# A hybrid SSD and attention layer: other places for the first conv's taps and softplus, the scan's tokens loaded ahead, the pre-norm's gains ahead of the first weights

## The chip, the cores and the metric

The kernel runs on one core of a Trainium2 chip. The core has a matrix engine (TensorE, PE), a vector engine (VectorE, DVE), a scalar engine (ScalarE, ACT), a general engine (GpSimd, POOL) and a queue engine (SyncE, SP) that here issues the transfers (DMAs). PEld is PE's loading of weights, which overlaps its matmuls. The metric is the device time of one execution in microseconds (us), as the median of several runs; lower is better. The clock in the profile is the one granted to TensorE, as a share of full speed.

## The reference

One layer on 16 learned meta tokens and 1024 tokens, width 1024, float32 throughout:

```python
h = concat([meta, x])
xn = rms_norm(h, mix_pre_g)
proj = xn @ w_in                      # z, xbc, dt_raw, q, k, v
y_ssd = ssd_mixer(z, xbc, dt_raw, ...)
y_sb = rms_norm(stick_breaking_attention(q, k, v), sb_norm_g)
h = h + rms_norm(concat([y_ssd, y_sb]) @ w_out, mix_post_g)
gu = rms_norm(h, ffn_pre_g) @ w_up
f = (gelu(causal_dwconv(gu[:DFF])) * gu[DFF:]) @ w_down
out = (h + rms_norm(f, ffn_post_g))[16:]
```

and in the mixer, which the change touches:

```python
xbc = silu(causal_dwconv(xbc, conv_w, conv_b))    # 4 taps; x (1024), B and C (2 groups of 128)
dt = softplus(dt_raw + dt_bias)
# over chunks of 128 tokens: y = (C.B^T * decay) @ (x dt) + C @ state,
# state = state * decay + B^T @ (x dt * decay), then y = (y + x*D) * silu(z)
```

## The kernel before

**Number format and products.** Every float32 operand is split into a high part (`h`, by a copy on ACT into the rounded matmul type) and a low part (`l`, the remainder, by a subtraction on POOL or DVE). Each product of two operands is then three matmuls, high by high, high by low, low by high.

**Stages.** The program runs through a head (normalise the tokens, turn them so that width lies on the partitions, and project B and C of group 0 and dt), a stage of projections in blocks, the scan over chunks, the attention, the output projection and the feed-forward part. PE's order, and with it that of DVE, ACT and POOL, is the order in which the code is written; SP is scheduled automatically in the stage of projections, and in written order in the head and the scan.

**The head** (L330 to L470). SP loads in order: the meta tokens `xt0`, `xt1`, the weights of B (`wr_B`, 512 KB), the pre-norm's gains spread over the partitions (`gpre`), `xt2`, `xt3`, and so on. For each tile of tokens `square` (ACT, L359) gives the sum of squares, `root` (POOL, L169 and L170) the factor `rs_pre`, `norm` (DVE, L369) the tile `xn`, and `turn_x` (PE, L383) its eight transposes `xtp`, which ACT copies (high part) and DVE subtracts (low part). `split_hi` (ACT, L415) and `split_lo` (DVE, L419) split B's weights between `norm(1)` and `square(2)`.

**The projections** (class `Duo`, L258 to L321). A duo is two blocks of 128 columns of the weights, for 1040 tokens, in Strassen's manner: seven products numbered 1, 6, 5, 7, 2, 3, 4 instead of eight, each of 24 matmuls (L308), in three banks of accumulators `dA`, `dX`, `dY`. Product 7 adds into the bank of product 6, product 3 into that of 5, product 2 into that of 1. After each product its bank is added or copied out to the raw tiles `craw`, by ACT for products 1 and 2 (L317), by DVE for the others (L320, "evacuation" below). The first duo is of x columns (`x`), then comes one of z, then x, z, then B and C of group 1, and so on. The first duo takes its products in the order 1, 5, 2, 6, 7, 3, 4. While a duo runs, the weights of the next one are made ready, each step behind a certain product: `split_1` (`whi1`, `wlo1`) behind 2, `split_22` (`ah`, `al`) behind 1, `sums` (four operations on POOL, L285 to L288) behind 6, `split_3` behind 7, `split_4` (`whi4`, `wlo4`) behind 3. In `split_w` (L178) the high part is on ACT, L181, and the low part on POOL, L182.

**Slots.** `slots` is a list of lists: what is in `slots[j]` is issued behind the j-th product of the running duo. In it go the work on B and C of group 0 and on dt: the four taps of the conv on DVE (tap 0 is the TENSOR_SCALAR of L505, taps 1 to 3 the SCALAR_TENSOR_TENSOR of L508) with a silu on ACT (L512) as fifth entry (`b0_taps`, `c0_taps`; tiles `cdB`, `cdC`), the turning of B into tokens by PE and ACT (`b0_turns`, L491 and L496), and the seven actions `dts`: loads of dt's parameters, `turn_dt` (PE, `tpd`), `soft_a` (softplus: e = exp on ACT, then s and s2 on DVE, L659 to L664), `soft_b` (its series on DVE), three decays and their stores. The last x operands `t2l`, `t3l` and `t4l` are split on DVE (L255) in the same time.

**The scan** (L1192 to L1230). There are 18 units, 9 chunks by 2 groups. Unit n computes the weights of unit n+1 and the outputs of unit n: `sg` (segment sums, PE L1070, from the loads `sl` and `sg`), `em` (ACT and later DVE and POOL L1100), `xdt` and `xw` (POOL, L1075 and L1080, from the token tile `xk`), `cb` (PE), `yf`, `st` (PE L1120, from `xw`), `yt` (PE L1136), and on DVE `xd` and `zk` (L1145, L1146), the outputs, which SP stores as `yd` (L1149). Projections of q and k (`pj_q`, `pj_k`, L218) fill PE between. At the head of each unit SP is given: stores of the q and k projections (`put_stores`, n < 2), the group's B and C (`load_state`, n = 0, 2, 6, 10), `zk` and `xd` of unit n+1 (L1056 and its like; a buffer of `zk` is free when its store as `yd` is done), `sl` and `sg` of unit n+3 (`load_bc`), and `xk` of unit n+2 (L1048).

Of the kernel before, what the change touches and what calls it, by code (L numbers as in the profile page):

```python
# [9 lines left out]
F32 = mybir.dt.float32  # L10
# [3 lines left out]
ALU = mybir.AluOpType  # L14
# [52 lines left out]
def tile_layer(ctx: ExitStack, tc: tile.TileContext, x, meta, rows, parts,  # L67
# [190 lines left out]
    class Duo:  # L258
# [13 lines left out]

        def split_22(self):
            h, l = (weight_rows(sa.tile([P, 5 * P], F32R, tag=f"a22{e}", name=f"a{e}{self.nm}", bufs=2), 4, OFF22)
                    for e in "hl")
            raw = self.r[1][:, HI4]
            nc.scalar.activation(h, raw, AF.Copy)
            nc.gpsimd.tensor_tensor(l, raw, h.bitcast(F32), op=ALU.subtract)
            self.w["a22"] = h, l
# [44 lines left out]
    with tc.tile_pool(name="pre", bufs=3, side="right") as pre:  # L324
# [13 lines left out]
        load_x(1)  # L338
        raws = {"B0": raw_of("B0", w_xbc[8])}
        gpre = row_bcast(pre, 0, D, "gpre")  # L340
        load_x(2)
        load_x(3)
        raw_dt = pre.tile([P, KB, 16], F32, tag="wdt", name="wr_dt", bufs=1)
# [81 lines left out]
        norm(1)  # L425
        split_hi("B0")
        split_lo("B0")
        square(2)
        root(2)
        norm(2)  # L430
        turn_x(0)
        square(3)
        root(3)
# [191 lines left out]
    def dt_acts():  # L625
# [30 lines left out]
        def soft_a():  # L656
            dtx = box["dtx"]
            e, s, s2 = box["e"], box["s"], box["s2"] = [t3(n) for n in ("e1", "s1", "s2")]
            nc.vector.scalar_tensor_tensor(e, dtx, -1.0, dtx, op0=ALU.mult, op1=ALU.min)  # L659
            nc.scalar.activation(e, e, AF.Exp)  # L660
            nc.vector.tensor_scalar(s, e, 2.0, None, op0=ALU.add)
            nc.vector.reciprocal(s, s)
            nc.vector.tensor_tensor(s, s, e, op=ALU.mult)
            nc.vector.tensor_tensor(s2, s, s, op=ALU.mult)  # L664
# [39 lines left out]
        def store():  # L704
            nc.sync.dma_start(out=dtkd, in_=dtk)

        return [[loads], [turn_dt], [soft_a], [soft_b], [lambda: decay(0)], [lambda: decay(1)],
                [lambda: decay(2), store, turn_acs]]
# [31 lines left out]
    def merged(*lists):  # L740
# [3 lines left out]
    dts = dt_acts()  # L744
    slots = [b0_taps[:2] + dts[0], b0_taps[2:4], b0_taps[4:], [], c0_taps[:2] + b0_turns[:1],
             c0_taps[2:4] + b0_turns[1:2], c0_taps[4:] + b0_turns[2:], dts[1]]
    for i, q in enumerate(duos):
# [3 lines left out]
        for j, m in enumerate((1, 5, 2, 6, 7, 3, 4) if i == 0 else (1, 6, 5, 7, 2, 3, 4)):  # L751
# [6 lines left out]
            if n is not None:  # L758
                if m == 1:
                    n.split_22()  # L760
                elif m == 6:
                    n.sums()
                elif m == 7:
                    n.split_3()
                elif m == 2:
                    n.split_1()
                elif m == 3:
                    n.split_4()
            elif m in (7, 2):
                v_split(1, int(m == 2))  # L770
# [6 lines left out]
        if i == 1:  # L777
            slots = merged(slots, [[], dts[2], [], dts[3], [], [], []]) + [dts[4], dts[5], dts[6]]
        if i == n_early:
# [220 lines left out]
    with tc.tile_pool(name="ssd", bufs=1, side="right") as sp:  # L1000
# [191 lines left out]
        for n, (g, c) in enumerate(units):  # L1192
            if n == 12:
                for d, u in zip(vcd, (vd, vdp)):
                    nc.sync.dma_start(out=d.rearrange("(t r) c -> t r c", r=NM),
                                      in_=u[P:].rearrange("(t r) c -> t r c", r=P)[:, :NM])
            if n < 2:
                put_stores()
            if n in (0, 2, 6, 10):
                load_state(n // 2 + 2, n // 2 + (4 if n else 3))  # L1200
            if n + 1 < len(units):
                load_zx(*units[n + 1])
            if n + 3 < len(units):
                load_bc(*units[n + 3])
            if n + 2 < len(units):
                load_x(*units[n + 2])
            nxt = chunk_weights(*units[n + 1]) if n + 1 < len(units) else None
# [1288 lines left out]
```

## Time and profile before

| what | us |
|---|---|
| median of three runs | 1659.45 |
| lowest, highest | 1658.90, 1659.69 |
| profiled execution | 1663.12 |
| its span | 1661.4 |
| PE busy in it | 1627.9 |
| stage 0 to 53 (head): length, PE busy | 53.0, 41.4 |
| stage 53 to 425 (projections) | 372.0, 366.5 |
| stage 425 to 640 (scan and around it) | 215.0, 206.8 |
| 640 to 1150 (attention and output) | 510.0, 508.0 |
| 1150 to 1660 (feed-forward) | 510.0, 505.3 |

Granted clock over the span: 0.997. The row of a timeline reads: start, duration, engine, line, operation, output and inputs, sizes, and in brackets the idle time of the engine before it and what ended that. "x22" stands for 22 instructions in one row; the times are of the whole group. Lines are those of the kernel before.

### The profile page before, as it was taken

What the parts mean: (1) busy time and instruction counts of PE and PEld (TensorE: products, weight loads), DVE (VectorE), ACT (ScalarE), POOL (GpSimd) and SP (SyncE); (2) the same over time, 40 slices, a digit from 0 to 9 for tenths busy, and PEclk for the clock granted to TensorE, in tenths of its full rate; (3) what the DMA queues carried; (4) which work ended last, traced back from release to release, by engine and by line L of the source; (5) the groups of instructions that cost most, each with busy time, mean ns of one, the idle gap of its engine ahead of it and who ended that gap; (6) DMA issues with size and microseconds to landing.
All of it is one profiled execution on the core that took longest, in us unless ns stands there. A gap on an engine that the chain in (4) does not pass through costs nothing.

```text
span 1661.4 us, 28993 instructions
## 1 busy us (share of the span) xinstructions
PE 1627.9 (98%) x11508; PEld 1433.2 (86%) x11508; DVE 1091.1 (66%) x1248; ACT 747.7 (45%) x1100; POOL 780.6 (47%) x579
## 2 busy tenths in 40 slices
PE   7999999999999999999999999999999999999998
PEld 6999999978777788888877889999999999888886
DVE  7975744344367689999840677766566655658877
ACT  7444344332234367767652435433333333344544
POOL 2876877520357463455431113777777767200001
PEclk9999999999999999999999999999999999999999
DMA  4543235334577776545254542232233332495335
GB/s 175 184 152 132 102 120 195 134 136 146 144 223 237 248 224 198 153 142 152 68 178 148 176 165 90 96 96 95 95 98 109 114 106 83 140 331 175 95 116 182
DMA packets 164518, 247.39 MB, mean 149 GB/s; under 512 B 18487, under 2 KB 99495, under 8 KB 162702
## 3 DMA queue, kind: packets, MB, share of 16 engines
q1 hardware_dynamic: 163806, 244.48, 45.8%
q8 instruction: 91, 1.49, 0.4%
q10 hardware_dynamic: 576, 1.05, 0.2%
q14 instruction: 45, 0.37, 0.1%
HBM read 161.99 MB, written 83.46 MB: 148 GB/s over the span
## 4 chain that ended last, share of the span: by engine, by line
PE 86%; DVE 4%; DMA 3%; POOL 3%; issue 2%; SPq 1%; ACT 1%; POOLq 0%; DVEq 0%; ACTq 0%
PE fX L1900 10%; PE mo L1504 10%; PE dnA L2312 7%; PE fY L1900 7%; PE fA L1900 7%; PE dnB L2312 5%; PE av L1352 3%; PE tw L1332 3%; PE z L1308 3%; DVE kp L1314 2%; PE dXz L308 2%; PE dXqk L308 2%; PE vA L819 2%; PE pj_q L218 2%; PE pj_k L218 2%
## 5 line engine op out<-in xcount | busy, mean ns | idle before, releaser
L1314 DVE TENSOR_TENSOR_SCAN kp<-kp,hold 128x396 f32<-128x396 f32 (+5 forms) x224 | 211.1, 1013 | 20.2 <-ACT kp L1309 18.3
L182 POOL TENSOR_TENSOR wlo<-wr,whi 128x1024 fp32r<-128x1024 f32 x43 | 99.3, 2318 | 41.0 <-ACT whi L181 41.0
L2349 POOL TENSOR_TENSOR fms<-fms 128x1 f32<-128x1 f32 x8 | 2.3, 287 | 222.0 <-DMA ar<-fda 185.9
L181 ACT ACTIVATE whi<-wr 128x1024 fp32r<-128x1024 f32 x43 | 45.7, 1063 | 112.2 <-PE fX L1900 73.5
L1972 DVE SCALAR_TENSOR_TENSOR ga<-gr,pp,ga 128x1024 f32<-128x1024 f32 x44 | 69.3, 1575 | 34.0 <-ACT ga L1965 33.2
L2234 ACT ACTIVATE dh<-ar 128x512 fp32r<-128x512 f32 x77 | 48.6, 631 | 94.7 <-PE dnB L2312 44.7
L2235 DVE TENSOR_TENSOR dl<-ar,dh 128x512 fp32r<-128x512 f32 x77 | 53.2, 691 | 47.1 <-ACT dh L2234 47.1
L1309 ACT ACTIVATE kp<-z 128x788 f32<-128x788 f32 (+4 forms) x96 | 72.7, 832 | 16.6 <-PE z L1308 12.2
L1337 ACT ACTIVATE th<-tw 128x1024 f32<-128x1024 f32 (+2 forms) x96 | 70.8, 813 | 15.6 <-PE tw L1332 15.6
L1352 PE MATMUL av<-th,v 128*64 128x128 f32 x1152 | 70.0, 275 | 2.0 <-POOL tmsa L985 0.9
L1332 PE MATMUL tw<-ident,kp 128*128 128x128 f32 x576 | 70.0, 276 | 0.8 <-DVE kp L1314 0.4
L1352 PEld LDWEIGHTS av<-th,v 128*64 128x64 f32 x1152 | 62.3, 137 | 8.1 <-issue 3.9
L1332 PEld LDWEIGHTS tw<-ident,kp 128*128 128x128 f32 x576 | 62.4, 141 | 8.0 <-issue 7.0
L2312 PE MATMUL dnA<-dl,dh 128*128 128x512 f32 x176 | 68.5, 389 | 0.0
L2312 PE MATMUL dnA<-dh 128*128 128x512 f32 x176 | 68.5, 389 | 0.0
L2312 PE MATMUL dnA<-dh,dl 128*128 128x512 f32 x176 | 68.5, 389 | 0.0
L1286 POOL TENSOR_SCALAR cb<-kp 128x32 f32<-128x32 f32 x64 | 42.9, 678 | 50.6 <-DVE kp L1314 44.3
L2033 POOL TENSOR_TENSOR al<-wr,ah 128x512 fp32r<-128x512 f32 x20 | 28.6, 1431 | 77.5 <-ACT ah L2032 77.4
L1308 PE MATMUL z<-k,q 64*128 64x396 f32 (+9 forms) x672 | 62.3, 329 | 1.0 <-DVE st L941 1.0
L1308 PEld LDWEIGHTS z<-k,q 64*128 64x128 f32 x672 | 53.1, 185 | 10.7 <-ACT th L1337 4.2
L2312 PE MATMUL dnB<-dh 128*128 128x512 f32 x132 | 51.3, 389 | 0.0
L2312 PE MATMUL dnB<-dh,dl 128*128 128x512 f32 x132 | 51.3, 389 | 0.0
(987 smaller groups left out, 6027.2 us busy)
## 6 DMA issues: line engine op xcount, KB each, us to landing
wr<-in_w_up SPq DMA_DIRECT2D x44, 512.0 KB
fds<-ga SPq DMA_DIRECT2D x44, 256.0 KB
b<-in_w_down SPq DMA_DIRECT2D x44, 256.0 KB
ar<-fds SPq DMA_DIRECT2D x44, 256.0 KB
fda<-ga SPq DMA_DIRECT2D x33, 256.0 KB
ar<-fda SPq DMA_DIRECT2D x33, 256.0 KB
k<-qkd SPq DMA_DIRECT2D x8, 1040.0 KB
q<-qkd SPq DMA_DIRECT2D x64, 128.0 KB
```

Source lines behind the costliest of these rows:

```text
L182: nc.gpsimd.tensor_tensor(l, raw, h.bitcast(F32), op=ALU.subtract)
L218: mm(acc[:, :CQ - s], a[:, k, :], b[:, k % 4, c + s:c + CQ], start=(k == 0 and j == 0), stop=(k == KB - 1 and j == 2))
L1308: mm(z[:, j, a - lo:e - lo], u[h, :], r[h, a - bases[x]:e - bases[x]], start=s_ == 0, stop=s_ == 2)
L1309: nc.scalar.activation(kp[:, :, lo:top], z[:, :, :top - lo], AF.Sigmoid, scale=-QSCALE)
L1314: nc.vector.tensor_tensor_scan(part, part, hold[:, L - last + a:L - last + e][:, ::-1], 1.0 if e == last else kp[:, j, e:e + 1], op0=ALU.m ...
L1332: nc.tensor.transpose(tw[:, j, b, :], kp[:, j, c0:c0 + P], ident)
L1337: copied[0] = nc.scalar.activation(th[:, :, :nb, :], tw[:, :, :nb, :], AF.Copy, scale=-1.0, bias=1.0).ins
L1352: mm(av[halves[j], 1 - x, :], v[:, kb, halves[j]], th[:, j, b, :], start=kb == 0, stop=kb == i)
L1504: recent[0] = mm(acc, u[:, k, :], v[:, cs], start=(k == 0 and j == 0), stop=(k == 7 and j == 2))
L1900: mm(acc[:, c, :nn], u[:, k, :], v[:, k, c0:c0 + nn], start=first and k == 0 and j == 0, stop=k == 3 and j == 2, skip_group_check=not first)
L1972: nc.vector.scalar_tensor_tensor(v, self.g[jj][:, :, i:i + 256], fconv_w[:, j, i:i + 1], v, op0=ALU.mult, op1=ALU.add)
L2312: mm(banks[BANK[n], t], u[:, 0, c], v[:, 1, :], start=(n in (1, 2, 5) and p == 0 and i == 0), stop=(p == NPR - 1 and i == 2), skip_group_c ...
```

## The change

There are five edits.

1. Head: on SP `gpre` and `xt2` are issued ahead of `wr_B`. ACT takes the split of `wr_B` (high) behind `square(2)`; DVE takes the low part behind `norm(2)` and `turn_x(0)`.
2. `split_22` has an engine argument. For the duo that is made ready while the first one runs (the first z duo), the low part `alz` goes to DVE; for the others it stays on POOL.
3. `slots`: the conv of B moves one product later, tap 2 alone behind the third product, tap 3 and silu behind the fourth, C's tap 0 alone behind the fifth, and so on. The loads of dt stay behind the first product.
4. `soft_a` keeps e and the exp; s and s2 become an action of their own (`soft_m`), one slot later, and `soft_b` follows one slot later than before.
5. Scan: `load_x(n+2)` and `load_bc(n+3)` are issued at the head of the unit, ahead of `put_stores`, `load_state` and `load_zx`.

```diff
-        def split_22(self):
+        def split_22(self, eng=nc.gpsimd):
...
-            nc.gpsimd.tensor_tensor(l, raw, h.bitcast(F32), op=ALU.subtract)
+            eng.tensor_tensor(l, raw, h.bitcast(F32), op=ALU.subtract)
...
-        raws = {"B0": raw_of("B0", w_xbc[8])}
         gpre = row_bcast(pre, 0, D, "gpre")
         load_x(2)
+        raws = {"B0": raw_of("B0", w_xbc[8])}
...
-        split_hi("B0")
-        split_lo("B0")
         square(2)
         root(2)
         norm(2)
+        split_hi("B0")
         turn_x(0)
+        split_lo("B0")
...
             nc.scalar.activation(e, e, AF.Exp)
+
+        def soft_m():
+            e, s, s2 = box["e"], box["s"], box["s2"]
             nc.vector.tensor_scalar(s, e, 2.0, None, op0=ALU.add)
...
-    slots = [b0_taps[:2] + dts[0], b0_taps[2:4], b0_taps[4:], [], c0_taps[:2] + b0_turns[:1],
-             c0_taps[2:4] + b0_turns[1:2], c0_taps[4:] + b0_turns[2:], dts[1]]
+    slots = [dts[0], b0_taps[:2], b0_taps[2:3], b0_taps[3:], c0_taps[:1], c0_taps[1:3] + b0_turns[:1],
+             c0_taps[3:] + b0_turns[1:2], b0_turns[2:] + dts[1]]
...
-                    n.split_22()
+                    n.split_22(nc.gpsimd if i else nc.vector)
...
-            slots = merged(slots, [[], dts[2], [], dts[3], [], [], []]) + [dts[4], dts[5], dts[6]]
+            slots = merged(slots, [[], dts[2], dts[3], [], dts[4], [], []]) + [dts[5], dts[6], dts[7]]
...
+            if n + 2 < len(units):
+                load_x(*units[n + 2])
+            if n + 3 < len(units):
+                load_bc(*units[n + 3])
             if n < 2:
                 put_stores()
             if n in (0, 2, 6, 10):
                 load_state(n // 2 + 2, n // 2 + (4 if n else 3))
             if n + 1 < len(units):
                 load_zx(*units[n + 1])
-            if n + 3 < len(units):
-                load_bc(*units[n + 3])
-            if n + 2 < len(units):
-                load_x(*units[n + 2])
```

How the order of the instructions changes is shown at three places.

DVE in the first duo, from the split `t2l` to the evacuation of product 6. `cdB` is the conv of B, `craw_x<-dYx` the evacuation of product 5 and `craw_x<-dXx` that of product 6, `alz` the low part of the z weights; before:

```order
L255 TENSOR_TENSOR t2l<-t2r,t2h 128x2080
L505 TENSOR_SCALAR cdB_851<-craw_B_256,pp 128x1040
L508 SCALAR_TENSOR_TENSOR cdB_851<-craw_B_256,pp,cdB_851 128x1040
L636 TENSOR_TENSOR fold<-ident 32x16
L255 TENSOR_TENSOR t3l<-t3r,t3h 128x2080
L320 TENSOR_TENSOR craw_x_838<-dYx_867,craw_x_838 128x520
L508 SCALAR_TENSOR_TENSOR cdB_851<-craw_B_256,pp,cdB_851 128x1040 x2
L320 TENSOR_TENSOR craw_x_840<-dXx_926,craw_x_838 128x520
```

The same stretch after the change:

```order
L255 TENSOR_TENSOR t2l<-t2r,t2h 128x2080
L255 TENSOR_TENSOR t3l<-t3r,t3h 128x2080
L278 TENSOR_TENSOR alz_848<-wrz_802,ahz_847 128x4x128
L636 TENSOR_TENSOR fold<-ident 32x16
L320 TENSOR_TENSOR craw_x_838<-dYx_864,craw_x_838 128x520
L505 TENSOR_SCALAR cdB_890<-craw_B_256,pp 128x1040
L508 SCALAR_TENSOR_TENSOR cdB_890<-craw_B_256,pp,cdB_890 128x1040 x2
L320 TENSOR_TENSOR craw_x_840<-dXx_923,craw_x_838 128x520
```

Taps 0 and 1 stood ahead of `t3l` and now stand behind the evacuation of product 5, tap 3 has gone behind the evacuation of product 6, and `alz` has come in ahead of that of product 5.

DVE in the third duo, around softplus, before. `e`, `s` and `dtx` are softplus's tiles, `craw_x<-dXx` and `craw_x<-dYx` the evacuations:

```order
L320 TENSOR_TENSOR craw_x_1351<-dXx_1364,craw_x_1349 128x520
L659 SCALAR_TENSOR_TENSOR e_1403<-dtx 128x144
L661 TENSOR_SCALAR s_1404<-e_1403 128x144
L662 RECIPROCAL s_1404<-s_1404 128x144
L663 TENSOR_TENSOR s_1404<-s_1404,e_1403 128x144
L664 TENSOR_TENSOR s_1405<-s_1404 128x144
L320 TENSOR_TENSOR craw_x_1349<-dYx_1412,craw_x_1349 128x520
```

And after:

```order
L320 TENSOR_TENSOR craw_x_1351<-dXx_1364,craw_x_1349 128x520
L659 SCALAR_TENSOR_TENSOR e_1403<-dtx 128x144
L320 TENSOR_TENSOR craw_x_1349<-dYx_1408,craw_x_1349 128x520
L664 TENSOR_SCALAR s_1404<-e_1403 128x144
L665 RECIPROCAL s_1404<-s_1404 128x144
L666 TENSOR_TENSOR s_1404<-s_1404,e_1403 128x144
L667 TENSOR_TENSOR s_1405<-s_1404 128x144
```

The evacuation into `craw_x` from `dYx` has moved from behind the four operations on `s` to ahead of them.

SP in the scan, the loads that one unit issues. `zk` and `xd` are of the next unit, `sl` and `sg` of the one three ahead, `xk` of the one two ahead, and `yd` is the store of this unit's output; before:

```order
L1056 DMA zk_1_4841<-zd_114 128x4x128
L1056 DMA xd_1_4843<-xdd_102 128x4x128
L1039 DMA sl_4471<-acsd 8x128
L1040 DMA sg_4472<-diagd_807 8x1024
L1039 DMA sl_4471<-acsd 8x128
L1040 DMA sg_4472<-diagd_808 8x1024
L1048 DMA xk_2_4849<-xsd_115 128x512
L1149 DMA yd_90<-zk_0_4656 128x4x2
```

The same unit after (lines are three further on; the rows with `bt`, `ct` and `bn` are `load_state`'s):

```order
L1051 DMA xk_2_4835<-xsd_115 128x512
L1042 DMA sl_4471<-acsd 8x128
L1043 DMA sg_4472<-diagd_807 8x1024
L1042 DMA sl_4471<-acsd 8x128
L1043 DMA sg_4472<-diagd_808 8x1024
L1017 DMA bt_4461<-bcd_596 128x256
L1018 DMA ct_4462<-bcd_597 128x256
L1021 DMA bn_4463<-bnd_600 128x256
L1017 DMA bt_4464<-bcd_598 128x256
L1018 DMA ct_4465<-bcd_599 128x256
L1021 DMA bn_4466<-bnd_601 128x256
L1059 DMA zk_1_4847<-zd_114 128x4x128
```

`xk`, `sl` and `sg` have moved from behind `zk` and `xd` to the head of the unit, ahead of the state's loads too.

More of the change, by code (lines that the diff above doesn't have):

```diff
@@ L705, in store @@
             nc.sync.dma_start(out=dtkd, in_=dtk)
-        return [[loads], [turn_dt], [soft_a], [soft_b], [lambda: decay(0)], [lambda: decay(1)],
+        return [[loads], [turn_dt], [soft_a], [soft_m], [soft_b], [lambda: decay(0)], [lambda: decay(1)],
                 [lambda: decay(2), store, turn_acs]]
```

## The prediction

> **What bounds the kernel now.** I read the page first: TensorE (PE) is busy nearly all the time, so only what opens or closes a gap on PE can change the time.
>
> ```profile
> span 1661.4 us, 28993 instructions
> PE 1627.9 (98%) x11508; PEld 1433.2 (86%) x11508; DVE 1091.1 (66%) x1248; ACT 747.7 (45%) x1100; POOL 780.6 (47%) x579
> ```
>
> 1661.4 - 1627.9 leaves 33.5 us of idle PE. The view of PE's waits (what PE waited for: us in total, times, longest) says where; these five lines are among those that the change can touch.
>
> ```profile
> PE xtp L383 <- DVE xn L369: 11.6, 5, 9.7
> PE st L1120 <- POOL xw L1080: 3.2, 2, 1.9
> ...
> PE dYx L308 <- DVE craw_x L320: 1.3, 1, 1.3
> PE dXz L308 <- POOL wlo4z L182: 1.0, 1, 1.0
> ...
> PE dXx L308 <- DVE craw_x L320: 1.0, 1, 1.0
> ```
>
> They are the head (xtp), three places in the first blocks of projections (dXx, dXz, dYx) and the scan (st): together 18.1 us, of which one wait of 9.7 is the start of the program. I then read the timeline of each engine around each place. The profiled execution took 1663.12 us: its span of 1661.4 and 1.7 around it. That is 3.67 above the median of the runs shown (1659.45). I add the terms to 1663.12 and then move the result down by 3.67.
>
> **The x block (products 5, 6, 7 of the first duo): a new stall.** The rows of DVE, then POOL, ACT and PE, each with start, duration, engine, line, operation, and in brackets the idle time before and what ended it:
>
> ```profile
> 58.24 0.81 DVE L505 TENSOR_SCALAR cdB<-craw_B,pp 128x1040 f32<-128x1040 f32 x1
> 59.09 1.30 DVE L508 SCALAR_TENSOR_TENSOR cdB<-craw_B,pp,cdB 128x1040 f32<-128x1040 f32 x1
> 60.39 2.31 DVE L255 TENSOR_TENSOR t3l<-t3r,t3h 128x2080 fp32r<-128x2080 f32 x1
> ...
> 63.23 4.78 DVE L508 SCALAR_TENSOR_TENSOR cdB<-craw_B,pp,cdB 128x1040 f32<-128x1040 f32 x2
> 67.93 0.69 DVE L320 TENSOR_TENSOR craw_x<-dXx,craw_x 128x520 f32<-128x520 f32 x1
> 70.98 2.53 DVE L255 TENSOR_TENSOR t4l<-t4l,t4h 128x2080 fp32r<-128x2080 f32 x1 [2.36 <-ACT t4h L254]
> 74.04 1.18 DVE L505 TENSOR_SCALAR cdC<-craw_C,pp 128x1040 f32<-128x1040 f32 x1
> ```
>
> ```profile
> 62.09 2.67 POOL L182 TENSOR_TENSOR wlo4x<-s24x,whi4x 128x1024 fp32r<-128x1024 f32 x1 [5.96 <-ACT whi4x L181]
> 64.71 2.20 POOL L278 TENSOR_TENSOR alz<-wrz,ahz 128x512 fp32r<-128x512 f32 x1
> 67.52 2.55 POOL L182 TENSOR_TENSOR wlo1z<-wrz,whi1z 128x1024 fp32r<-128x1024 f32 x1
> 70.03 1.29 POOL L285 TENSOR_TENSOR wrz<-wrz 128x512 f32<-128x512 f32 x1
> 71.40 3.26 POOL L286 TENSOR_TENSOR wrz<-wrz,wrz 128x512 f32<-128x512 f32 x1
> ```
>
> ```profile
> 64.79 1.05 ACT L181 ACTIVATE whi1z<-wrz 128x1024 fp32r<-128x1024 f32 x1
> ```
>
> ```profile
> 68.67 0.39 PE L308 MATMUL dXx<-t3h,whi3x 128*128 128x260 f32 x1 [0.96 <-DVE craw_x L320]
> ```
>
> Read the ends against each other. wlo4x ends at 62.09 + 2.67 = 64.76, and alz, half as large, at 64.71 + 2.20 = 66.91. The two taps of 1.30 in the open (the row at 59.09) take 4.78 here. If the first ran only after 64.76 and the second only after 66.91, each needs about 1.1: 65.86, then 68.01, and 63.23 + 4.78 = 68.01. In the other direction, L286 starts at 71.40 and takes 3.26, while L285 with the same size took 1.29; t4l ends at 70.98 + 2.53 = 73.51, and 73.51 + 1.15 = 74.66, where L286 ends. So DVE and POOL take turns, a whole instruction at a time, and a record's duration includes the wait for the other. In turns a tap is 1.10 and tap 0 about 0.56; POOL's 512-wide operations take 1.15, its 1024-wide ones 2.06 (64.76 less t3l's end, 60.39 + 2.31 = 62.70). The Trainium skill, "SBUF — State Buffer", section "Who interferes with whom", says that a DVE instruction with two SBUF inputs, or in a two-port mode, and a GpSimd instruction that reads SBUF hold a shared pair of ports exclusively, the loser blocking for the whole instruction; it speaks against this change, and the trace agrees at 71.40 (3.26 against 1.29). By that page a one-input tap 0 outside the two-port modes would not wait, which would take one POOL turn, 1.15, off the stall below. The row at 74.04 (1.18 against 0.81 at 58.24) looks like waiting, so I keep it in.
>
> The change takes taps 0 and 1 (0.81 and 1.30 us, with POOL idle) from 58.24 to 60.39 and puts taps 0, 1, 2 between the evacuations of products 5 and 6, where POOL has three operations queued. It also puts alz on DVE ahead of product 5's evacuation. Step by step: wlo4x still ends at about 64.76, since it waits for ACT and then has its turn; alz on DVE to 65.3; product 5's evacuation (0.69) to 66.0; wlo1z, ready since whi1z at 64.79 + 1.05 = 65.84, takes the next turn at 65.95, 2.06, to 68.0; tap 0 to 68.6; L285, 1.15, to 69.75; tap 1 to 70.85; L286 to 72.0; tap 2 to 73.1; product 6's evacuation, 0.69, to 73.8, where it was 67.93 + 0.69 = 68.62. Product 7 adds into the bank that this evacuation reads, so PE starts it at 73.9 instead of 68.67: **+5.2**. If tap 0 gets ahead of wlo1z, one 1.15 less; if one more POOL operation gets in, one 1.15 more: 4.1 to 6.3.
>
> **The clock.** A gap can cost more than itself. Here are the only wait of the z block, the same matmuls in the chain of work that ended last (start, us, work), the stretch of 86 to 90 us (length; busy us of PE, PEld, DVE, ACT, POOL; then granted clock, DMA share, GB/s), and the POOL operation waited for.
>
> ```profile
> 84.97 0.58 PE L308 MATMUL dXz<-t2h,wlo4z 128*128 128x260 f32 x1 [1.03 <-POOL wlo4z L182]
> ```
>
> ```profile
> 84.97 4.35 PE dXz L308 x22
> 89.32 2.88 PE dYz L308 x24
> ```
>
> ```profile
> 86.00:90.00 4.00, 4.00 (x26) 4.00 (x26) 2.40 (x2) 0.00 (x0) 3.84 (x3) 0.72 0.37 146
> ```
>
> ```profile
> 81.73 3.18 POOL L182 TENSOR_TENSOR wlo4z<-s24z,whi4z 128x1024 fp32r<-128x1024 f32 x1
> ```
>
> 22 matmuls should take 2.88 x 22/24 = 2.64 and took 4.35: the clock was below full after the wait, for 1.71. The idle time in the x block grows from 0.96 to 6.2, so I charge it one such window: **+1.7** (0 to 3.4). In exchange, PE reaches product 6 of z about 6.9 us later, at 83.94 + 6.9 = 90.8, and wlo4z, at 84.91 before and one POOL turn later now, is long done: **-1.03** and **-1.71**. If PE is not later, both stay.
>
> **Softplus.** In the third duo, again of x columns, PE waits for an evacuation on DVE:
>
> ```profile
> 121.34 0.39 PE L308 MATMUL dYx<-b22h,whi4x 128*128 128x260 f32 x1 [1.26 <-DVE craw_x L320]
> ```
>
> That evacuation stands behind soft_a's s chain, which waits for ACT's exp; now it stands ahead of the chain, so the 1.26 goes: **-1.26** (0 to -1.26). The one slot by which soft_b moves is hidden: decay follows it by a slot as before. Sum of the projection blocks: 5.2 + 1.7 - 1.03 - 1.71 - 1.26 = **+2.9**.
>
> **The head.** DVE's first two norms, ACT's square of x2, and PE's fourth set of transposes:
>
> ```profile
> 8.34 2.47 DVE L369 SCALAR_TENSOR_TENSOR xn<-xt,rs_pre,gpre 16x1024 f32<-16x1024 f32 x2 [6.21 <-DMA gpre<-in_rows]
> ```
>
> ```profile
> 9.58 1.06 ACT L359 ACTIVATE junk<-xt 128x1024 bf16<-128x1024 f32 x1 [2.03 <-DMA xt<-in_x]
> ```
>
> ```profile
> 16.30 1.97 PE L383 MATMUL xtp<-ident,xn 128*128 128x128 f32 x8 [0.28 <-DVE xn L369]
> ```
>
> Transfers land in the order of issue, gpre just before 8.34 and x2 just before 9.58, 1.24 apart. Without B's weights ahead of them both come one such step sooner, B two steps later. ACT, which was done with B's split before x2 came, now splits B behind the square, in its place, so ACT is free at the same time as before; DVE's norm of x2 no longer stands behind B's split. The transposes at 16.30 come sooner by at most 1.24, and half of such a gain is lost while the clock has not come up: **-0.7** (0 to -1.24).
>
> **The scan.** SP's waits between 440 and 570 us, the issue of one xk load, POOL, and the four waits of PE:
>
> ```profile
> SPq L1056 <- DMA yd<-zk: 30.0, 12, 4.7
> ```
>
> ```profile
> 447.87 0.35 SPq L1048 DMA_DIRECT2D xk<-xsd  x1
> ```
>
> ```profile
> 450.66 1.04 POOL L1075 TENSOR_TENSOR xdt<-xk,dtk 128x512 f32<-128x512 f32 x1 [5.06 <-DMA xk<-xsd]
> ```
>
> ```profile
> 449.74 0.70 PE L1070 MATMUL sg<-sg,sl 32*128 32x512 f32 x2 [1.31 <-DMA sg<-diagd]
> 452.87 1.13 PE L1120 MATMUL st<-xw,bn 128*128 128x512 f32 x2 [1.38 <-POOL xw L1080]
> ...
> 470.26 1.86 PE L1120 MATMUL st<-xw,bn 128*128 128x512 f32 x2 [1.86 <-POOL xw L1080]
> ```
>
> ```profile
> 571.96 0.44 PE L1136 MATMUL yt<-em,xdt 128*64 128x128 f32 x4 [0.93 <-POOL em L1100]
> ```
>
> SP's zk load (L1056) waits for the store of the zk that lay in its buffer, 2.5 us each in twelve units, and the loads of sl, sg and xk for later units stand behind it. xk arrives at 450.66, 5.06 us after POOL was free; xdt, xw and PE's st follow from it. Ahead of the zk load these transfers go out earlier than POOL's 5.06 needs, at most by one unit. Then 1.31, 1.38, 1.86 and 0.93 (the last through POOL's later em) go. At 470.26 the clock fell as well, which these lines of the chain show against the unit before:
>
> ```profile
> 458.76 0.69 PE pj_q L218 x6
> 461.16 0.86 PE st L1120 x2
> ...
> 472.54 1.30 PE pj_q L218 x6
> ```
>
> st took 1.86 instead of 0.86, pj_q 1.30 instead of 0.69: 1.61. Together 7.1. Against it, the zk, xd and state loads go out behind 0.35 us each of some six moved issues, about 2 us, and what waits for them next may take a part; I take 1.0 off: **-6.1** (-3.0 to -7.1).
>
> **Sum.** -0.7 + 2.9 - 6.1 = -3.9. 1663.12 - 3.9 = 1659.2 for a profiled execution, and 1659.45 - 3.9 = **1655.5** for the timed runs. A measurement of this kernel can tell 0.2%, 3.3 us, from no change: faster is below 1656.1, slower above 1662.8.
>
> **The rivals.**
> - *The clock windows do not hang on the waits.* The two windows (1.71 and 1.61) are together 3.3 of the 3.67 by which the profiled execution exceeds the median, so the timed runs may have had neither. Then removing the waits recovers only the waits: blocks 5.2 + 1.7 - 1.03 - 1.26 = +4.6, scan -6.1 + 1.6 = -4.5, head -0.7: -0.6, **1658.9**, no change. Against it: in the trace both windows begin at a wait. The Trainium skill, "TensorE: Matmul & The Clock Gate", "Part 1: The HAM clock gate", puts the half clock behind at least one idle window of about 3.4 us, in free-running windows; by it a 1.03 us wait would not have done it, and this rival's sum would hold. The trace differs at 84.97, where the clock fell at a wait of 1.03. Chance 0.24.
> - *The scan's wait only changes its name.* zk, xd or state become the last to arrive, and the gain is 2.5 (sg's 1.31 and the half of 452.87 and 571.96, 1.2): -0.7 + 2.9 - 2.5 = -0.3, **1659.1**. For it: SP's 30.0 us of waiting stays. Against: DVE uses zk and xd a unit after they are loaded. Chance 0.11.
> - *The taps do not take turns with POOL*, because they come before wlo1z, L285 and L286 are ready: 66.0 + 0.81 + 1.30 + 1.30 + 0.69 = 70.1, so product 7 starts 1.4 later, not 5.2, and the clock holds: 1.4 - 1.03 - 1.71 - 1.26 = -2.6 for the blocks, -0.7 - 2.6 - 6.1 = -9.4, **1650.1**. For it: wlo1z's release (65.84) and tap 0's (66.0) lie 0.2 apart. Against: once one of the two has gone, the rows at 70.98 and 71.40 show strict turns. Chance 0.12.
> - *Slower: the backlog stays.* DVE and POOL do not catch up after the x block, and wlo4z comes later than 90.8, 5 us more than I give it; then z waits again and the clock falls there and at softplus too: 5.2 + 3 x 1.7 + 1.0 = +11.3, less 0.7 and 6.1: +4.5, **1664.0**. For it: POOL was busy 3.84 of 4.00 us from 86 to 90. Against: DVE was idle for 2.36 before 70.98, which takes up half of it. Chance 0.13.
>
> **How the numbers follow.** The forecast has 0.40; with the stall and its clock at their low ends (blocks 4.1 - 4.0 = +0.1) it gives 1652.7, at their high ends (6.3 + 3.4 - 4.0 = +5.7) 1658.3, with the scan at -7.1 1654.5 and at -3.0 1658.6; I put 0.29 of it below 1656.1 and 0.11 within 0.2%. The first rival adds 0.04 to faster and 0.20 to no change, the second 0.11 to no change, the third 0.12 to faster, the last 0.13 to slower. Faster 0.45, same 0.42, slower 0.13. The range leaves out half of the third (0.06) and the last (0.13): 1650.0 to 1661.0.
>
> **What would show it.** Right: PE's list of waits has dXx on craw_x near 6 us at about 68 us, product 6's evacuation ends near 73.8 behind three taps that each end 1.1 after a POOL operation, dXz no longer waits for wlo4z, dYx at 121 no longer for craw_x, and st no longer for xw. Wrong: a dXx wait below 3 us, st still waiting for xw or a new wait of yt or DVE on zk and xd, or PE's head wait longer than 11.6.

## The result and the profile after

The changed kernel took 1664.89 us (median of 7 runs, 1662.89 to 1666.25), the kernel before 1659.73 in the same comparison: a ratio of 1.0025, with a 95% interval from 1.0015 to 1.0036; measured once more later, 1.0014 (experiment 10). By the prediction's threshold of 0.2% the first is slower and the second no change. The forecast was 1655.5, in a range of 1650.0 to 1661.0: too low, and of the wrong sign. The changed kernel's profiled execution took 1666.25 us with a span of 1664.5, 3.1 more than before.

The page and PE's waits after (what PE waited for: us in total, times, longest):

```profile
span 1664.5 us, 28994 instructions
PE 1630.4 (98%) x11508; PEld 1437.3 (86%) x11508; DVE 1089.7 (65%) x1249; ACT 747.9 (45%) x1100; POOL 778.5 (47%) x578
```

```profile
PE xtp L383 <- DVE xn L369: 11.3, 5, 8.5
PE dXx L308 <- DVE craw_x L320: 5.0, 1, 5.0
PE tpd L649 <- ACT xtkB L497: 2.9, 1, 2.9
PE yt L1139 <- DVE xd L1148: 1.5, 1, 1.5
```

The waits of st on xw, of sg, of dXz on wlo4z and of dYx are gone. Three have come or grown: dXx from 1.0 to 5.0, which the prediction had; tpd on ACT's copy of B's turned tokens, 2.9, which it had not; yt on xd, 1.5. PE's idle time is 1664.5 - 1630.4 = 34.1 us, and was 33.5. So in these two executions the waits cancel, and the difference is in PE's busy time: 2.5 us more for the same matmuls, of which 6.8 us more ran at half clock. Two stretches at half clock, with PE's granted clock as third number from the end:

```profile
72.00:77.00 5.00, 3.79 (x20) 3.79 (x21) 5.00 (x4) 0.00 (x0) 5.00 (x2) 0.66 0.00 0
89.00:100.00 11.00, 9.85 (x46) 9.78 (x47) 4.36 (x5) 2.60 (x5) 7.56 (x5) 0.54 0.23 96
```

A clock of 0.66 over 5.00 us is 2 x 0.34 x 5.00 = 3.4 us at half; 0.54 over 11.00 is 10.1 (10.2 summed over single us). Before, there were 3.4 us from 84.8 to 88.2 and 3.4 from 470.5 to 473.9.

By stage, from PE's timeline (first matmul of the first duo, dAx; first matmul of the decays, pz, at the end of the third duo; the scan's yt of 573.15 in the kernel before): the head ends at 55.07 instead of 54.54, +0.5; from there to pz 84.02 instead of 75.66, +8.4; from pz to yt 436.93 instead of 442.95, -6.0; the rest +0.2. The sum is +3.1.

**The x block.** DVE, POOL and PE after:

```profile
63.08 2.68 DVE L278 TENSOR_TENSOR alz<-wrz,ahz 128x512 fp32r<-128x512 f32 x1
...
65.77 0.68 DVE L320 TENSOR_TENSOR craw_x<-dYx,craw_x 128x520 f32<-128x520 f32 x1
66.38 0.80 DVE L505 TENSOR_SCALAR cdB<-craw_B,pp 128x1040 f32<-128x1040 f32 x1
67.21 5.34 DVE L508 SCALAR_TENSOR_TENSOR cdB<-craw_B,pp,cdB 128x1040 f32<-128x1040 f32 x2
72.47 0.69 DVE L320 TENSOR_TENSOR craw_x<-dXx,craw_x 128x520 f32<-128x520 f32 x1
```

```profile
62.59 2.62 POOL L182 TENSOR_TENSOR wlo4x<-s24x,whi4x 128x1024 fp32r<-128x1024 f32 x1 [5.95 <-ACT whi4x L181]
...
66.43 2.80 POOL L182 TENSOR_TENSOR wlo1z<-wrz,whi1z 128x1024 fp32r<-128x1024 f32 x1 [0.59 <-ACT whi1z L181]
69.19 2.26 POOL L285 TENSOR_TENSOR wrz<-wrz 128x512 f32<-128x512 f32 x1
```

```profile
73.21 0.59 PE L308 MATMUL dXx<-t3h,whi3x 128*128 128x260 f32 x1 [5.04 <-DVE craw_x L320]
```

alz ends at 65.76, 0.55 after wlo4x (65.21). Tap 0 got ahead of wlo1z (the 1.15 less that the prediction allowed for), then taps and POOL take turns: wlo1z to 69.23, tap 1, L285 to 71.45, tap 2 to 72.55, and product 6's evacuation ends at 73.16. The prediction had 73.8.

**ACT and tpd.** The wait that was missed:

```profile
88.55 1.07 ACT L512 ACTIVATE cdC<-cdC 128x1040 f32<-128x1040 f32 x1 [6.78 <-DVE dtx L651]
89.52 0.58 ACT L497 ACTIVATE xtkB<-tt_B 128x512 f32<-128x512 f32 x1
```

```profile
83.38 0.60 PE L496 MATMUL tt_B<-ident,cdB 128*128 128x128 f32 x4
86.69 0.60 PE L496 MATMUL tt_B<-ident,cdB 128*128 128x128 f32 x4
90.15 3.75 PE L649 MATMUL tpd<-fold,sq 32*16 32x16 f32 x18 [2.87 <-ACT xtkB L497]
```

PE turned the second part of B at 83.38, and ACT's copy of it ran only at 89.52, because C's silu stands ahead of it on ACT and waited for DVE's last tap of C (88.51). tpd needs a buffer of PSUM that this copy frees. tpd then ran at half clock and took 3.75; at full clock (before, at 81.41) it took 2.09.

**The scan.** xk comes in time, and xd has taken its place, which DVE now waits for in the unit with the six loads of the state:

```profile
476.95 0.69 DVE L1148 TENSOR_TENSOR xd<-yt,xd 128x512 f32<-128x512 f32 x1 [6.21 <-DMA xd<-xdd]
```

### The profile page after: what moved, and what is told of

It is laid out like the page before. It is cut to its first block, busy times and chain, and to the rows that moved or that the text cites. A ratio compares the mean times of both kernels' runs of the same rounds, so it can differ in the third digit from the quotient of the medians.

```text
span 1664.5 us, 28994 instructions
## 1 busy us (share of the span) xinstructions
PE 1630.4 (98%) x11508; PEld 1437.3 (86%) x11508; DVE 1089.7 (65%) x1249; ACT 747.9 (45%) x1100; POOL 778.5 (47%) x578
## 4 chain that ended last, share of the span: by engine, by line
PE 60%; DVE 2%; issue 1%; POOL 1%; ACT 0%; DMA 0%; SPq 0%; POOLq 0%; DVEq 0%; ACTq 0%
PE fX L1903 10%; PE mo L1507 10%; PE dnA L2315 7%; PE fY L1903 7%; PE fA L1903 7%; PE dnB L2315 5%; PE av L1355 3%; PE tw L1335 3%; PE z L1311 2%; DVE kp L1317 2%; PE g0a L1917 1%; PE x2tp L1781 0%; PE pj_k L218 0%; PE g0d L1917 0%; PE g0c L1917 0%
## 5 line engine op out<-in xcount | busy, mean ns | idle before, releaser
L1975 DVE SCALAR_TENSOR_TENSOR ga<-gr,pp,ga 128x1024 f32<-128x1024 f32 x44 | 69.3, 1575 | 34.1 <-ACT ga L1968 33.3
L2238 DVE TENSOR_TENSOR dl<-ar,dh 128x512 fp32r<-128x512 f32 x77 | 53.2, 691 | 47.2 <-ACT dh L2237 47.2
L1312 ACT ACTIVATE kp<-z 128x788 f32<-128x788 f32 (+4 forms) x96 | 72.7, 832 | 16.3 <-PE z L1311 11.6
```

The lines of the kernel that those rows point to most:

```text
L1312: nc.scalar.activation(kp[:, :, lo:top], z[:, :, :top - lo], AF.Sigmoid, scale=-QSCALE)
L1975: nc.vector.scalar_tensor_tensor(v, self.g[jj][:, :, i:i + 256], fconv_w[:, j, i:i + 1], v, op0=ALU.mult, op1=ALU.add)
L2238: sub(lo[:, k], raw, hi[:, k].bitcast(F32), op=ALU.subtract)
```

## The experiments

Theory 1 says: DVE's taps and POOL's operations take turns in the first two duos, which makes dXx wait; ACT's copy of the second turn stands behind C's silu, which makes tpd wait; and each gap may bring stretches of half clock. Theory 2 is in each case the rival named there. Ratios are to the kernel before in the same comparison.

**1. Old slots, alz on POOL** (edits 2 and 3 undone).

```diff
-    slots = [dts[0], b0_taps[:2], b0_taps[2:3], b0_taps[3:], c0_taps[:1], ...
+    slots = [b0_taps[:2] + dts[0], b0_taps[2:4], b0_taps[4:], [], ...
-                    n.split_22(nc.gpsimd if i else nc.vector)
+                    n.split_22()
```

> The changed kernel with the old slots and the z weights' low part alz back on POOL; the head, the later s chain of softplus and the scan's loads as changed. Theory 1 (DVE and POOL take turns in the first duo, and the copy of B's turned tokens stands behind C's silu on ACT): the 5.0 us wait of dXx and the 2.9 us wait of tpd go, and the four stretches of half clock behind them; what is left is the head's +0.5, softplus's -1.4 and the scan's -4.5 to -6.1: 1653 to 1656 us beside 1659.7 for the kernel before and 1664.9 for the change. Theory 2 (the clock windows lie where the free-running grid puts them, the waits recover only themselves): 4.5 + 2.9 = 7.4 us recovered at most, 1657 to 1659.

Measured: 1655.54 us, ratio 0.9962 (0.9950 to 0.9974). Both new waits are gone, and nothing of the projections ran at half clock in the profiled execution, which was the fastest of the five (1653.67). The old wait of dXz is back, without half clock behind it:

```profile
83.29 0.39 PE L308 MATMUL dXz<-t2h,wlo4z 128*128 128x260 f32 x1 [1.05 <-POOL wlo4z L182]
```

```profile
84.00:88.00 4.00, 4.00 (x36) 4.00 (x35) 3.86 (x3) 0.00 (x0) 3.84 (x3) 1.00 0.48 187
```

So edits 1, 4 and 5 gain 6.3 us (0.38% by the ratio; the medians lie 5.2 apart) together, and edits 2 and 3 lose more than that.

**2. Only alz back on POOL** (the second pair of lines above).

> The changed kernel with alz back on POOL and the new slots kept. Theory 1: product 5's evacuation on DVE no longer stands behind alz, but alz takes a turn of POOL among the taps: tap 0 ends at 65.3, tap 1 at 67.6, tap 2 at 70.7, product 6's evacuation at 71.4 instead of 73.2, so the wait of dXx falls from 5.0 to about 3.3 and the rest stays: 1663. Theory 2: alz's engine does not matter, since DVE's order and not the turns makes the stall: 1664.9 and a wait of dXx of 5.0.

Measured: 1665.03 us, ratio 1.0022 (1.0013 to 1.0031), no different from the change's 1.0025. In the profile the turns came as reckoned, and gave it back elsewhere:

```profile
PE dXx L308 <- DVE craw_x L320: 3.6, 1, 3.6
PE tpd L649 <- ACT xtkB L497: 3.3, 1, 3.3
...
PE dAx L308 <- ACT craw_x L317: 1.3, 1, 1.3
```

dXx 1.4 less, tpd 0.4 and dAx 0.7 more. The mechanism of theory 1 held, its time did not: as long as tpd waits for the end of C's taps, an earlier arrival of PE is waited away there. Experiment 7 tests this.

**3. The second turn of B ahead of C's silu.**

```diff
-             c0_taps[3:] + b0_turns[1:2], b0_turns[2:] + dts[1]]
+             b0_turns[1:2] + c0_taps[3:], b0_turns[2:] + dts[1]]
```

> The changed kernel with one pair exchanged in the slots: the second turn of B (PE transposes and ACT's copy) is issued ahead of C's last tap and silu, not behind them. Theory 1: ACT's copy no longer waits for DVE's tap 3 of C through the silu, tpd's wait of 2.9 us goes, and with it most of the 10 us of half clock behind it (1.7 us on tpd, about 3 on the products of z): 1657 to 1660. Theory 2: the clock falls because tpd's eighteen small matmuls keep PE lightly loaded, so only the wait goes: 1662.

Measured: 1660.67 us, ratio 1.0002 (0.9992 to 1.0012): 0.12% to 0.23% below the change in its two comparisons, and the interval of the second (1.0005 to 1.0022) overlaps this one. tpd no longer waits and runs at full clock; ACT copies behind the transposes, ahead of the silu:

```profile
84.70 0.60 ACT L497 ACTIVATE xtkB<-tt_B 128x512 f32<-128x512 f32 x1 [2.24 <-PE tt_B L496]
88.21 1.07 ACT L512 ACTIVATE cdC<-cdC 128x1040 f32<-128x1040 f32 x1 [2.90 <-DVE dtx L651]
```

```profile
87.92 2.09 PE L649 MATMUL tpd<-fold,sq 32*16 32x16 f32 x18
```

This exchange of two entries brings the kernel back to even. The time lies between the two theories (1657 to 1660, and 1662); the profile, where all half clock behind tpd is gone, is with theory 1. Theory 2's reason is not refuted by it: experiment 7 has the same order and 3.4 us of half clock behind tpd, without a wait. dXx still waits 5.0, and 6.8 us behind it ran at half clock.

**4. The scan's loads as before** (edit 5 undone in the changed kernel).

> The changed kernel with the scan's loads in the old order. Theory 1: the loads ahead are worth 6.1 us in the trace, of which up to 1.6 is a stretch of half clock that not every execution has: 1669.4 to 1671. Theory 2: the waits of the scan depend on where the grid of clock windows and the stores fall, which the 9 us delay from the projections moves too, so the old order costs less than 3 here: 1665 to 1668.

Measured: 1667.21 us, ratio 1.0037 (1.0025 to 1.0049), 0.12% to 0.23% more than the change, 2 to 4 us: the time is in theory 2's range, and the interval overlaps that of the change's first comparison. The waits did come back, and the scan from pz to yt took 441.45 us, 4.5 more than in the change:

```profile
PE st L1123 <- POOL xw L1083: 1.9, 2, 1.5
...
PE sg L1073 <- DMA sg<-diagd: 1.5, 1, 1.5
```

**5. The scan's loads ahead alone** (edit 5 in the kernel before).

> The kernel before with the scan's loads ahead and nothing else. Theory 1 (the loads ahead are worth what PE waited for in the scan, less the new wait of yt on xd): PE's waits of 1.3 on sg, 3.2 on xw and 0.9 on em go, one of 1.5 to 2.0 on xd comes: -3.4 to -4, or -5 where a stretch of half clock fell there: 1655.5 to 1657.5 beside 1660.75. Theory 2 (the wait only changes its name, as the 2 us that the old order cost in the changed kernel suggest): -2, 1658.5 to 1660.

Measured: 1658.39 us, ratio 0.9978 (0.9969 to 0.9986): -3.7 us, within -2.3 to -5.1, which is theory 1's (the medians lie 3.0 apart, between the theories). The scan took 437.11 from pz to yt, 5.8 less than before; in this profile 6.8 us of half clock behind the scan gave back 2 of it. The two kernels at the same work (clock third from the end):

```profile
590.00:598.00 8.00, 7.11 (x61) 6.27 (x58) 6.38 (x9) 2.73 (x6) 5.68 (x7) 0.57 1.09 341
```

```profile
596.00:604.00 8.00, 7.11 (x84) 6.62 (x83) 6.38 (x9) 3.87 (x8) 6.55 (x8) 1.00 1.07 325
```

The first is of the scan alone, the second of the kernel before. Of 12 profiles with the loads ahead five have such a stretch between 586 and 603 us, and experiment 11 has one in the scan, at 447; the two in the old order have one in the scan, at 470 and 457, and none behind it.

**6. Softplus and scan, without the head** (edits 4 and 5 alone).

> The kernel before with the s chain of softplus behind the evacuation and the scan's loads ahead; head, slots and alz as before. Against the run that has the changed head as well (1655.5): theory 1 (the head's change gains what PE's wait for xn loses, 1.2, and the grid of clock windows decides from run to run whether it is seen): 1656 to 1657.5. Theory 2 (the head's change costs 0.5, as in the profile of the change, since ACT's copies of the first turn come 0.6 later): 1655.

Measured: 1658.98 us, ratio 0.9982 (0.9973 to 0.9990). The head's edit, which is what experiment 1 has more than this, is then worth 0.20%, 3.3 us with some 2.5 either way: the sign of theory 1, and the 1.2 of its waits lies within; the time is above its range. Softplus's 1.3 doesn't show beside experiment 5: from dAx to pz the profiles took 74.0 and 74.2, and dYx waits in neither of them, although experiment 5 has softplus in the old order.

**7. The second turn first, and alz on POOL.**

> The changed kernel with the second turn of B ahead of C's silu, as in the run before with 1660.7, and with alz on POOL too. Theory 1 (alz on POOL does shorten the wait of dXx, by 1.4, and the run with alz alone showed nothing because tpd waits for the end of C's taps whenever PE gets there): with that wait gone the 1.4 is seen: 1659 to 1659.5. Theory 2 (alz on POOL takes from dAx what it gives to dXx): 1660.5 or more.

Measured: 1659.35 us, ratio 0.9984 (0.9975 to 0.9993): 0.18% below experiment 3, 3 us with some 2 either way. dXx waits 3.6, tpd not at all, and 3.4 us of half clock behind tpd came without a wait. Theory 1 forecast the time; dAx still takes its 0.7 back (1.3), so 0.7 of the 3 us is shown as waits; what the rest is stays open.

**8. Old slots, alz on POOL, the state's loads last.**

```diff
             if n + 3 < len(units):
                 load_bc(*units[n + 3])
+            if n + 1 < len(units):
+                load_zx(*units[n + 1])
             if n < 2:
                 put_stores()
...
-            if n + 1 < len(units):
-                load_zx(*units[n + 1])
```

> The run with the old slots and alz on POOL (1655.5), with one more exchange in the scan: the loads of zk and xd stand ahead of put_stores and of the state's six loads. Theory 1: xd, which DVE waited 4.8 to 6.2 us for in the unit with the state's loads, comes 2.5 us sooner, yt's wait of 1.4 on xd goes: 1654. Theory 2: zk's wait for its buffer now holds up the state's loads, and PE waits for those instead, as much or more: 1655.5 to 1658.

Measured: 1655.12 us, ratio 0.9960 (0.9946 to 0.9973), the same as experiment 1. yt's wait is gone and a wait of 0.8 on sg stands in its place: half of theory 1, half of theory 2.

**9. Without POOL's four sums for the first z duo.** That part of z is then not what the reference has.

```diff
             r1, r2 = self.r
+            if self.i == 1:
+                self.s24 = r1
+                return
```

> The changed kernel without the four sums on POOL for the first z duo (L285 to L288; its second pair of operands is then made from the raw first block, so this part of z is not the reference's). Theory 1 (DVE's taps wait for POOL a turn at a time): tap 2 of B has no turn of L285 ahead of it, so product 6's evacuation ends 1.0 to 1.2 sooner and the wait of dXx falls from 5.0 to about 4; four turns fewer stand among tap 3 of B and the taps of C too, so C's silu comes about 4 us sooner and tpd's wait of 2.9 is gone: 1658 to 1661 beside 1664.9. Theory 2 (the length of DVE's own list makes both waits): dXx 5.0, tpd 2.9, 1664.9.

Measured: 1661.94 us, ratio 1.0004 (0.9995 to 1.0014); the change in the same comparison 1.0014, and the intervals overlap; the time is above theory 1's range. The taps' record falls by 0.89 from 5.34, for the one turn of L285, and later ones stand alone:

```profile
65.80 4.45 DVE L511 SCALAR_TENSOR_TENSOR cdB<-craw_B,pp,cdB 128x1040 f32<-128x1040 f32 x2
...
73.01 1.30 DVE L511 SCALAR_TENSOR_TENSOR cdB<-craw_B,pp,cdB 128x1040 f32<-128x1040 f32 x1
```

dXx waits 4.2, as theory 1 said, though not a row of DVE was moved: the turns are shown. tpd still waits 1.8, since C's taps still wait for wlo3z and wlo4z. That the edit shortened this wait at all is not shown: in experiment 4, whose projections are the change's, it is 1.8 too, with the half clock in the same pieces as here (6.8 behind dXx, 3.4 behind tpd).

**10. The change once more.**

> The changed kernel once more, unedited. Theory 1 (the waits are fixed by the order, the stretches of half clock by where a grid of 3.41 us windows happens to lie): waits of dXx 5.0 and tpd 2.9 within 0.5, the half clock again in whole multiples of 3.41 us but not the same number of them at the same places (four in the first profile, one behind dXx and three behind tpd). Theory 2 (a wait of a given length always brings the same stretch): the same 3.4 and 10.2 us at the same places. Time by both: 1663 to 1666.

Measured: 1663.34 us, ratio 1.0014 (1.0005 to 1.0022). The waits are 5.0 as before and 2.5 instead of 2.9, within theory 1's 0.5; the half clock is as long in total and lies otherwise:

```profile
68.00:76.00 8.00, 4.42 (x23) 4.43 (x24) 7.96 (x5) 1.42 (x2) 7.84 (x4) 0.57 0.11 44
89.00:96.00 7.00, 7.00 (x34) 6.96 (x34) 3.94 (x4) 0.97 (x2) 6.20 (x5) 0.51 0.35 141
```

8.00 x 2 x 0.43 and 7.00 x 2 x 0.49 are 6.9 each: two of 3.41 behind either wait, where the first profile had one and three. Theory 1.

**11. alz on DVE behind product 5, B's tap 3 and silu behind product 6** (otherwise as 8).

```diff
-                if m == 1:
-                    n.split_22()
+                if m == (1 if i else 5):
+                    n.split_22(nc.gpsimd if i else nc.vector)
...
-    slots = [b0_taps[:2] + dts[0], b0_taps[2:4], b0_taps[4:], [], c0_taps[:2] + b0_turns[:1],
+    slots = [b0_taps[:2] + dts[0], b0_taps[2:3], [], b0_taps[3:], c0_taps[:2] + b0_turns[:1],
```

> The run with the old slots, alz on POOL and the state's loads last (1655.1), with alz on DVE again, but behind product 5 instead of product 1, and with B's tap 3 and silu behind product 6 instead of 5 and 2. Theory 1: DVE does tap 2 ahead of wlo1z and then product 6's evacuation without a longer wait, POOL saves alz's turn of about 1.2 and reaches wlo4z sooner by that, so the wait of dXz (1.0) goes and with it the stretch of half clock that followed it: 1652.5 to 1654.5. Theory 2: tap 3 and t4l then hold up the evacuation of product 7 and PE waits there instead: 1655 to 1657.

Measured: 1658.40 us, ratio 0.9983 (0.9973 to 0.9993), above both theories. dXz no longer waits, and neither theory named what does: B's first turn, one product behind its silu, for that silu.

```profile
PE tt_B L491 <- ACT cdB L512: 3.7, 1, 3.7
```

**12. The same, with B's turns a product later, ahead of C's taps.**

```diff
-    ... b0_taps[3:], c0_taps[:2] + b0_turns[:1], c0_taps[2:4] + b0_turns[1:2], c0_taps[4:] + b0_turns[2:], dts[1]]
+    ... b0_taps[3:], c0_taps[:2], b0_turns[:1] + c0_taps[2:4], b0_turns[1:2] + c0_taps[4:], b0_turns[2:] + dts[1]]
```

> The last run's kernel (alz on DVE behind product 5, tap 3 of B and its silu behind product 6), with B's turns where the change has them, one product later, but each ahead of C's taps and silu of its slot. Theory 1 (what is left of the last run's loss is one wait, of B's first turn for its silu on ACT, 3.7 us, and the half clock that follows it): that wait goes, tpd does not wait, dXz does not wait for wlo4z, and nothing else comes: 1652 to 1654.5, ratio to the kernel before 0.994 to 0.996. Theory 2 (DVE and POOL have so much to do in the first two duos that a wait taken away at one place comes back at the next): some other wait of 1 us or more on PE between 60 and 100 us, 1655 to 1658.

Measured: 1655.06 us, ratio 0.9965 (0.9951 to 0.9978). The waits are theory 1's, the time lies 0.6 above its range. The longest wait of PE between 53 and 130 us is 0.9, of tt_B on that silu; dXz, dYx, tpd do not wait. Half clock there is all the same, with no wait ahead of it, only tpd, eighteen matmuls of 32x16:

```profile
81.09 2.09 PE L649 MATMUL tpd<-fold,sq 32*16 32x16 f32 x18
```

```profile
83.00:87.00 4.00, 4.00 (x21) 3.97 (x21) 3.31 (x7) 2.57 (x4) 1.52 (x1) 0.57 0.40 163
```

It is no faster than experiments 1 and 8 by more than the intervals; these three are the fastest versions tried, and beat both kernels.

The first three duos (dAx to pz) and the half clock in them, in us. Each row is one execution; those of experiments 1 and 12 were the fastest of their five.

| kernel | dAx starts | dAx to pz | at half clock |
|---|---|---|---|
| before | 54.5 | 75.7 | 3.4 |
| change | 55.1 | 84.0 | 13.7 |
| 10, change again | 53.4 | 82.7 | 13.7 |
| 1, old slots, alz on POOL | 52.9 | 72.7 | 0 |
| 2, alz on POOL | 54.4 | 82.4 | 10.2 |
| 3, second turn first | 54.6 | 77.9 | 6.8 |
| 4, scan as before | 53.9 | 81.7 | 10.2 |
| 5, scan alone | 54.9 | 74.2 | 3.4 |
| 6, softplus and scan | 55.4 | 74.0 | 3.4 |
| 7, second turn first, alz on POOL | 53.2 | 77.6 | 6.8 |
| 8, state last | 54.7 | 74.2 | 3.4 |
| 9, no sums | 53.7 | 80.7 | 10.2 |
| 11, alz behind 5 | 53.2 | 78.1 | 6.8 |
| 12, turns late | 53.4 | 73.8 | 3.4 |

## Why the prediction was wrong

**The x block** was right in its mechanism and near in size: product 7 started 4.5 later where +5.2 was reckoned, the wait grew by 4.1, and the order of turns was the one given, with tap 0 ahead. Experiment 9 shows POOL's turns in it.

**The step that failed** is the one behind it: "PE reaches product 6 of z about 6.9 us later ... wlo4z ... is long done", as if nothing else stood on that way. wlo4z was done, at 85.6, but PE came there 9.9 later, at 93.8. The edit moves B's turns and C's taps too, and these were followed on DVE, not on ACT. ACT runs in order; the copy that frees tpd's buffer had come behind C's silu, which waits for a tap that the turns with POOL had made late. That wait, +2.9, had no term. Experiment 3 shows the cause: one exchange takes the wait away, and the kernel is back at 1.0002. The second step that failed is the clock's term, which was put at nothing net.

**The clock** was charged with one window at the x block and paid back with one at z, a net of nothing. It cost 8.4 - (4.1 + 2.9 - 1.0 - 1.3) = 3.7 us, for 13.7 us at half clock instead of 3.4; PE's busy time in the three duos, 75.20 instead of 71.42, grew by 3.8. (Three windows more at the prediction's 1.7 each would be 5.1; part of them lay over idle time of PE, and the rest of the difference stays open.) The forecast tied one window to each wait. The first rival was right that they do not hang together so closely. Every wait of dXx or tpd of 1.8 us and more was followed by one to three windows, but not by the same number: 2.9 by three in one execution, 2.5 by two in another. yt's wait of 2.5 in experiment 10 brought none. The wait of dXz, 1.0 to 1.1 with tpd ahead of it, brought one in the kernel before and in experiments 5, 6 and 8, and none in experiment 1. Experiments 7, 11 and 12 have half clock at this place with no wait at all, behind tpd alone, so what the kernel before lost there need not have been wlo4z's.

The Trainium skill, "TensorE: Matmul & The Clock Gate", "Part 1: The HAM clock gate", has the window as free-running. The trace agrees in so far as the stretches here are all whole multiples of 3.4 us. The same section of the Trainium skill has the half clock come after an idle window of about 3.4 us. The traces differ: 2.09 us of small matmuls were enough, and in the scan a wait of 1.86.

**The sum.** In the blocks +8.4 was measured where +2.9 was reckoned: of the 5.5 between, 3.7 is the clock and 2.9 tpd's wait, less 1.1 by which dXx's wait grew less than reckoned. The head adds 1.2, so the profile came out 7.0 above the forecast's -3.9. In the timed runs the miss is 2.3 more, 9.3. Of that, 2.0 is because the two profiled executions are not alike: the one before lay 3.4 above its median, the one after 1.4 above its own, while the prediction moved its result down by 3.67. The last 0.3 is the median before, 1659.73 over all seven runs instead of 1659.45 over three.

**Softplus** came out as reckoned, dYx's wait of 1.26 is gone in the change, but no run shows that edit 4 took it away. It is gone in experiment 5 too, whose code is that of the kernel before up to the scan. The last operation on `s`, and POOL beside it, in the kernel before:

```profile
118.50 2.18 DVE L664 TENSOR_TENSOR s<-s 128x144 f32<-128x144 f32 x1
```

```profile
118.33 2.19 POOL L182 TENSOR_TENSOR wlo3z<-wrz,whi3z 128x1024 fp32r<-128x1024 f32 x1
```

And in experiment 5:

```profile
118.17 0.31 DVE L664 TENSOR_TENSOR s<-s 128x144 f32<-128x144 f32 x1
```

```profile
118.69 2.19 POOL L182 TENSOR_TENSOR wlo3z<-wrz,whi3z 128x1024 fp32r<-128x1024 f32 x1 [0.73 <-ACT whi3z L181]
```

Where wlo3z came first, the operation took 2.18 instead of 0.31. So the 1.26 looks like one more turn with POOL, which one execution had and the other had not. The prediction took it for a fixed cost of the order.

**The head** was right in size on the average, with a spread as large as the gain, and not in the profile that was shown: dAx started 0.5 later there. Over the eleven profiles with the new head, dAx starts between 52.9 and 55.1, at 53.8 on the mean, and between 54.5 and 55.4 in the three with the old one: -1.1 against -0.7 reckoned.

**The scan** was right in the profile, -6.0 against -6.1, with yt's wait on xd (1.5, where 1.0 was taken off) as the part that comes back; the prediction's own list of signs counts such a wait as wrong. In the timed runs it is worth 3.7 (experiment 5), and 2 to 4 in the changed kernel (experiment 4): 1.6 of the 6.1 was a window of half clock which not every run need have, and in five of twelve profiles a window fell behind the scan instead. Whether these two make up the whole difference is not settled.

**The slower rival** came within a microsecond of the time, 1664.0, by luck and not by its mechanism: wlo4z was done at 85.6, and product 6 of z came at 93.8. It had three windows of half clock, and the extra wait of PE, at another place.

## What to carry to other kernels

When an edit moves a step by one slot, go through every in-order engine that the step uses and ask what now stands ahead of it there, and what that waits for: here the costly one was a copy of 0.6 us on an engine that is 45% busy. If two engines take turns, a short operation behind three of the other engine's is as late as all of them together; place it where the other engine is idle. And count a gap on PE, or a stretch of tiny matmuls, with the clock behind it, by a range: how many windows follow a gap changes from run to run, so one profile does not give the price.

## What the runs showed of the hardware

The half clock of TensorE came in whole multiples of 3.4 us (3.4, 6.8, 10.2), behind waits of 1.5 to 5.0 us and behind 2.1 us of small matmuls without a wait (tpd in experiment 12; eighteen of 128x1 at 587 us in experiment 5), and the same program had them in different pieces in two executions. The same eighteen of 128x1 brought none in the kernel before (at 594.85), so these runs show no rule for when it comes. The kernel before was timed between 1657.6 and 1664.8 in the runs that were compared, a spread of 0.4%. Only one execution of it was profiled, so how much of the spread is half clock, and how much turns as at softplus, stays open.

DVE's tap 0, with a single tensor input from SBUF, also waits its turn. In the change, with POOL's L288 running until 79.26:

```profile
78.63 1.19 DVE L505 TENSOR_SCALAR cdC<-craw_C,pp 128x1040 f32<-128x1040 f32 x1
```

```profile
77.08 2.18 POOL L288 TENSOR_TENSOR s24z<-wrz,s24z 128x512 f32<-128x512 f32 x1
```

With POOL idle, at 58.24 in the kernel before, tap 0 took 0.81. At 66.38 in the change it took 0.80 because it went first; there POOL's wlo1z waited: it took 2.80, of which 2.05 lie behind tap 0's end at 67.18.
